# Transposes of the softmax statistics: one per step, and eight steps into the next unit for the last pair

## Chip, cores and metric

The kernel runs on one core of one Trainium2 chip. The metric is the device time of one execution in microseconds (us), median of the runs of one kernel; lower is better. The engines are named as in the profile: PE (TensorE) multiplies matrices, PEld loads its weights, DVE (VectorE), ACT (ScalarE) and POOL (GpSimd) work on tiles, SP issues the DMA transfers.

## What is computed

One layer of a decoder trunk on x (2048 rows of 1024). After an RMS norm, one input projection gives queries, keys, values, memory queries and a gate. Twelve heads of 64 in three groups attend to a dilated window each, (128, 1), (512, 4) and (2048, 16); four memory heads attend to 256 memory rows. The three groups are merged by the shares of their softmax denominators:

```python
# per group g: o (heads' outputs) and lse (log-sum-exp) of the window's scores
alpha = jax.nn.softmax(jnp.stack(lses, axis=0), axis=0)
mixed = [(outs[g] * alpha[g][..., None]) for g in range(3)]
# (mixed heads ++ memory heads) * silu(gate) -> output projection -> residual -> RMS norm
```

So for every row and head the merge needs two numbers of each group: the score's negated maximum and the sum of the exponentials. The kernel keeps them for all heads in two small tiles, `nm_all` and `l_all`.

## The kernel before

The rows are cut into four chunks of 512 (c = 0 to 3). The heads go in pairs of 64 + 64; the order is two pairs of heads of groups 2, 1, 1, 0, 0, then the stage of the memory heads, and at the end the last pair, (2,1). A pair and a chunk make a unit: the projections K, V, Q and gate one after the other, then a burst of scores and values. Each projection is 24 products of 128x512 (eight slices of the depth, three products per slice because the operands are split in a high and a low part: lines 142, 143, 144). A memory unit has only Q and gate. After the last pair comes the output phase: 16 blocks of rows, each two output projections (lines 706 to 708).

The emission is timed by steps. `run()` counts one slot for every `yield` of the projection that is being emitted; a projection is four steps of six products, so a unit is 16 steps and a memory unit 8. `at(n, f)` puts work f into the slot n later, and `steps(gen)` lets a generator go on by one part, up to its next `yield`, per slot. A tile framework then decides the final order on each engine from these emissions; all waits come from it: an instruction waits for its operands and for a free buffer. The buffers that matter are three PSUM banks `pp` (projections and transposes share them), four banks `ps` for scores, one bank `po` for values, one SBUF tile `mid` through which blocks are turned, four `p` for probabilities.

Every engine works off its own queue in order. What the change and the prediction touch:

- Scores: L401 (memory: L457) to `ps`. L379 on DVE subtracts the bias and writes a column of `nm_all`; L380 on ACT takes the exponentials and writes a column of `l_all` (memory: L462, L466, L469, then L473 on POOL). The probabilities are turned by L335 on DVE through `mid`, L338 (DMA to `t_dr`) and L344 (DMA back to `p`), and then read by the values' products, L423 or L446, into `po`. L426 takes `po` out.
- Values: V is evacuated from `pp` by L251, turned by L323 through the same `mid` and by copies L326 on ACT and POOL into `vb`. K and Q are evacuated by L251 (L290 for memory), the gate by L312.
- `shares()` is started 20 slots into the memory stage. For the six pairs done by then it transposes each group's columns of `nm_all` and `l_all` on PE into a `pp` bank (L584), copies the bank to SBUF on DVE (L586), writes it to `st_dr` in DRAM in a new order (L591, L593, L596), reads it back (L601), works out the shares in `weigh_groups` (L561 to L574) and stores them in `f_dr` (L607).
- `chunk_shares(c)` does the same for the last pair and one chunk: two transposes (L616), two copies (L617), stores (L622), a read (L629), `weigh_groups`, stores to `f_dr` (L635). It runs in the unit after the chunk's own, for the last chunk in the output phase.
- `make_y` multiplies the heads' outputs by `f_dr` (read L671, product L675, split L676 and L677) for the output products.

Of the kernel before, what the change touches and what calls it, by code (L numbers as in the profile page):

```python
# [34 lines left out]
def trunk_kernel(ctx, tc, xT, xrows, w_in, g_in, w_out, memT, mrows, g_mem, w_mem, g_fin, nbias, ident_in, out):  # L35
# [33 lines left out]
    def sb(shape, dt, tag, bufs):  # L69
        return pool.tile(shape, dt, tag=tag, name=f"{tag}_{nc.next_id()}", bufs=bufs)  # L70

    def tmp():
        return sb([P, CH], F32, "tmp", 3)

    def pbank(p=ps_p, tag="pp"):
        return p.tile([P, CH], F32, tag=tag, name=f"{tag}_{nc.next_id()}")
# [5 lines left out]
    def w_tiles():  # L82
        return sb([P, NK, P], F32R, "wh", 4), sb([P, NK, P], F32R, "wl", 4)
# [475 lines left out]
    def weigh_groups(m, f):  # L559

        v.tensor_tensor(f[:, 3, :], m[:, 0, :], m[:, 2, :], op=ALU.min)  # L561
        v.tensor_tensor(f[:, 3, :], f[:, 3, :], m[:, 4, :], op=ALU.min)
        for g in range(3):
            v.tensor_tensor(f[:, g, :], f[:, 3, :], m[:, 2 * g, :], op=ALU.subtract)
        yield
        a.activation(f[:, :3, :], f[:, :3, :], AF.Exp)
        yield
        for g in range(3):
            v.tensor_tensor(m[:, 2 * g, :], f[:, g, :], m[:, 2 * g + 1, :], op=ALU.mult)
        v.tensor_tensor(m[:, 0, :], m[:, 0, :], m[:, 2, :], op=ALU.add)  # L570
        v.tensor_tensor(m[:, 0, :], m[:, 0, :], m[:, 4, :], op=ALU.add)
        v.reciprocal(m[:, 0, :], m[:, 0, :])
        for g in range(3):
            v.tensor_tensor(f[:, g, :], f[:, g, :], m[:, 0, :], op=ALU.mult)  # L574

    def shares():

        kk = sb([P, 5 * P], F32, "kk", 2)
        vb = sb([P, 5, P], F32, "vb", 2)
        for i, src in enumerate((nm_all, l_all)):  # L580
            for g in range(3):
                n = 32 if g == 2 else 64
                pt = pbank()
                pe.transpose(pt[:n, :P], src[:, g, :n // 16].rearrange("p h b -> p (h b)"), ident)  # L584
                t = (vb[:64, 3 * i + g, :] if 3 * i + g < 5 else kk[:64, :P])
                v.tensor_copy(t[:n], pt[:n, :P])  # L586
                for h in range(n // 16):
                    dst = st_dr[2 * g + i, h]
                    s = t[16 * h:16 * h + 16, :]
                    if g == 2:  # L590
                        sp.dma_start(dst.rearrange("(r n) -> r n", r=16), s)  # L591
                    elif g == 1:
                        sp.dma_start(dst.rearrange("(j b i) -> b j i", j=4, b=16),  # L593
                                     s.rearrange("b (j i) -> b j i", j=4))
                    else:
                        sp.dma_start(dst.rearrange("(r b i) -> b r i", r=16, b=16),  # L596
                                     s.rearrange("b (r i) -> b r i", r=16))
            yield
        q = S // 32
        m = kk[:64, :6 * q].rearrange("p (s n) -> p s n", s=6)  # L600
        sp.dma_start(m, st_dr[:, :2].rearrange("s h (b n) -> (h b) s n", n=q))  # L601
        for _ in range(4):
            yield
        f = vb.rearrange("p b n -> p (b n)")[:64, :4 * q].rearrange("p (s n) -> p s n", s=4)
        yield from weigh_groups(m, f)
        yield
        sp.dma_start(f_dr[:, :2].rearrange("g h (b n) -> (h b) g n", n=q), f[:, :3, :])  # L607
        yield

    def chunk_shares(c):  # L610

        cs = slice(c * CH, (c + 1) * CH)
        t = tmp()
        for i, src in enumerate((nm_all, l_all)):
            pt = pbank()
            pe.transpose(pt[:32, :P], src[:, 2, 2:].rearrange("p h b -> p (h b)"), ident)  # L616
            v.tensor_copy(t[:32, i * P:(i + 1) * P], pt[:32, :P])  # L617
        yield
        for i in range(2):
            for h in range(2):  # L620
                b = 16 * h + 4 * c
                sp.dma_start(st_dr[4 + i, 2 + h, cs].rearrange("(r n) -> r n", r=4), t[b:b + 4, i * P:(i + 1) * P])  # L622
        q = CH // 32
        m = t[:64, 2 * P:2 * P + 6 * q].rearrange("p (s n) -> p s n", s=6)
        f = t[:64, 3 * P:3 * P + 4 * q].rearrange("p (s n) -> p s n", s=4)
        for _ in range(2):
            yield
        for h in range(2):
            sp.dma_start(m[32 * h:32 * h + 32], st_dr[:, 2 + h, cs].rearrange("s (b n) -> b s n", n=q))  # L629
        for _ in range(3):  # L630
            yield
        yield from weigh_groups(m, f)
        yield
        for h in range(2):
            sp.dma_start(f_dr[:, 2 + h, cs].rearrange("g (b n) -> b g n", n=q), f[32 * h:32 * h + 32, :3, :])  # L635
        yield
# [46 lines left out]
    def load_rows(r):  # L683
        residual[r] = row_tile("wh")
        sp.dma_start(residual[r], xr[r])
# [54 lines left out]
    def at(delay, fn):  # L740
        todo.setdefault(slot[0] + delay, []).append(fn)
# [7 lines left out]
    def steps(gen):  # L749

        def step():
            if next(gen, 0) != 0:
                at(1, step)
        at(1, step)
# [56 lines left out]
    for idx, (g, pp) in enumerate(pairs):  # L811
        if g == 3:
            ws = memory_stage()
            continue
        col = 2 * g + pp
        nbs = {}

        def load_bias(col=col):
            nbs[0] = sb([P, CH], F32, "nb", 1).rearrange("p (h k) -> p h k", h=2)
            sp.dma_start(nbs[0], nbias[col])  # L820

        if idx == 0:
            ws = [w_tiles(), w_tiles()]
            first = load_early(0)
            for k in range(NK):
                next(first)
                if k % 2 == 0:
                    load_first(ws, (6 + col, 12 + col), k // 2)
            next(first, None)
            sp.dma_start(ident, ident_in)  # L830
            ws += [load_w(w_in[t]) for t in (col, 20 + col)]
            load_bias()
        else:
            at(7, load_bias)
        following = []
        if idx < 4:
            n = 2 * pairs[idx + 1][0] + pairs[idx + 1][1]
            ahead = [6 + n, 12 + n, n, 20 + n]
        else:
            ahead = [None, 26, 18, 27]  # L840
        prev = None
        for c in range(NC):
            st = {}
            pv = prev if g == 0 else None
            if idx == 6:
                if c == 0:
                    at(6, burst)
                else:
                    at(3, lambda c=c: steps(chunk_shares(c - 1)))
                if c == 1:  # L850
                    for i in range(2 * NK):
                        at(15 * i // 8, lambda i=i: load_wo(i))
                elif c == 3:
                    for k in range(NK):
                        at(2 * k, lambda k=k: make_y(0, k))
                    for i, fn in ((6, lambda: load_rows(0)), (10, load_gfin), (11, lambda: load_rows(1))):
                        at(i, fn)

            def load_ahead():
                if c == NC - 1 and idx < 5:  # L860
                    t = ahead[len(following)]
                    following.append(load_w(w_in[t]) if t is not None else None)

            if idx == 0 and c == 0:
                first_chunk(st, ws)
            else:
                if idx == 0 and c < NC - 1:
                    steps(load_x(c + 1))
                    at(14, lambda c=c: spread_r(c + 1))
                    at(17, lambda c=c: spread_r(c + 1))  # L870
                run(proj_k(st, g, c, ws[0], pv, late=4 if (idx, c) == (0, 1) else 0))
                if (idx, c) == (4, 3):
                    steps(memory_kv(mem))
                elif (idx, c) == (4, 1):
                    steps(memory_squares(mem))
                load_ahead()
                run(proj_v(st, g, c, ws[1], pv))
                load_ahead()
                run(proj_q(st, g, c, ws[2]))
                load_ahead()  # L880
            run(proj_gate(st, g, c, ws[3], ps=st.get("gate")))
            load_ahead()
            burst((st, g, pp, c), 1, nbs[0])
            prev = st
        ws = following
    at(2, lambda: steps(chunk_shares(3)))
    for c in range(NC):
        for b in range(4):
            if c < NC - 1:
# [67 lines left out]
```

## Time and profile before

| what | value |
| --- | --- |
| time, median of 3 runs | 991.27 us (990.44 to 993.23) |
| profiled execution | 994.41 us, its span 992.3 us |
| TensorE clock granted, mean | 0.99 of full speed |
| PE busy | 961.4 us, 97% of the span |
| DVE, ACT, POOL busy | 44%, 33%, 24% |

A busy share of 97% on PE leaves little idle time in all, and the map of the profile by 40 slices shows where it is: one slice near 720 to 744 us has PE busy 60% at a granted clock of 0.7. The list of waits tells for each line what PE waited for, and the timelines show the instructions around it. A row of a timeline gives the start, the time it took, engine, line, operation and tiles, and in brackets the idle time before it and what ended it.

### The profile page before, as it was taken

The page shows a single profiled execution, that of the slowest core. Times are in us where ns is not written, and L with a number is a line of the kernel's source. Part 1 is how long each engine was busy: PE and PEld are TensorE (multiplying, and loading weights), DVE is VectorE, ACT ScalarE, POOL GpSimd, SP SyncE. Part 2 cuts the span into 40 slices and gives each one's busy share as a digit, 9 for nine tenths or more (in the row PEclk, how much of TensorE's full clock was granted, in tenths as well). Part 3 has the DMA queues.
Part 4 walks back from the last instruction along what each step waited for, and adds up shares of the span by engine and source line. Part 5 has one row for each costly group of instructions (what it writes and reads, how often), then busy time and mean ns, then how long its engine had stood idle before and what let it go on. Part 6 is the DMA issues. An engine that isn't in the chain of part 4 may idle for free. (4 is left out here: it accounts for less than half of the span.)

```text
span 992.3 us, 13998 instructions
## 1 busy us (share of the span) xinstructions
PE 961.4 (97%) x4844; PEld 755.5 (76%) x4844; DVE 436.8 (44%) x1059; ACT 326.0 (33%) x996; POOL 242.6 (24%) x393
## 2 busy tenths in 40 slices
PE   7899999999999999999999999999969999999997
PEld 5677778888788777777777876777747778888886
DVE  7866433333333333433433334543434555556333
ACT  5756422233223322233323332222333441222111
POOL 4411500032002311131112255344431310111000
PEclk9999999999999999999999999999979999999999
DMA  5565322243224423354235543333562575876311
GB/s 190 164 202 181 118 84 85 75 139 128 85 86 125 142 85 96 98 136 129 86 96 163 176 130 117 129 138 117 174 212 84 161 226 161 258 226 195 127 64 63
DMA packets 104117, 135.17 MB, mean 136 GB/s; under 512 B 31856, under 2 KB 65904, under 8 KB 104048
## 3 DMA queue, kind: packets, MB, share of 16 engines
q1 hardware_dynamic: 104048, 134.30, 42.8%
q8 instruction: 38, 0.62, 0.3%
q14 instruction: 31, 0.25, 0.1%
HBM read 89.14 MB, written 45.12 MB: 135 GB/s over the span
## 5 line engine op out<-in xcount | busy, mean ns | idle before, releaser
L142 PE MATMUL pp<-xH,wh 128*128 128x512 f32 x888 | 359.3, 405 | 0.1
L143 PE MATMUL pp<-xL,wh 128*128 128x512 f32 x888 | 354.8, 400 | 2.4 <-DVE xL L200 2.4
L144 PE MATMUL pp<-xH,wl 128*128 128x512 f32 x888 | 354.5, 399 | 1.1 <-DVE wl L80 1.1
L142 PEld LDWEIGHTS pp<-xH,wh 128*128 128x128 f32 x888 | 168.4, 190 | 49.0 <-issue 9.3
L143 PEld LDWEIGHTS pp<-xL,wh 128*128 128x128 f32 x888 | 168.4, 190 | 44.9 <-DVE xL L200 3.7
L144 PEld LDWEIGHTS pp<-xH,wl 128*128 128x128 f32 x888 | 168.2, 189 | 44.5 <-DVE wl L80 2.4
L326 POOL COPY vb<-mid 32x128 f32<-32x128 f32 (+1 forms) x208 | 60.6, 291 | 234.8 <-DVE mid L323 226.6
L326 ACT COPY vb<-mid 32x128 f32<-32x128 f32 (+1 forms) x208 | 60.7, 292 | 155.8 <-DVE mid L323 153.7
L706 PE MATMUL pp<-xH 128*128 128x512 f32 (+1 forms) x264 | 101.1, 384 | 0.2 <-ACT xH L676 0.2
L707 PE MATMUL pp<-xL,xH 128*128 128x512 f32 (+1 forms) x264 | 101.0, 383 | 0.0
L708 PE MATMUL pp<-xH,xL 128*128 128x512 f32 (+1 forms) x264 | 100.9, 384 | 0.0
L380 ACT ACTIVATE p<-p,nm_all 128x128 f32<-128x128 f32 (+1 forms) x192 | 86.2, 450 | 43.3 <-DVE nm_all L379 27.4
L80 POOL TENSOR_TENSOR wl<-wraw,wh 128x512 fp32r<-128x512 f32 x52 | 67.1, 1302 | 125.9 <-ACT wh L79 123.8
L335 DVE STREAM_TRANSPOSE mid<-p 128x1024 f32<-128x1024 f32 (+1 forms) x56 | 66.9, 1194 | 47.5 <-DMA t_dr<-mid 36.1
L473 POOL TENSOR_SCALAR p<-p,sm 128x256 f32<-128x256 f32 x64 | 58.2, 928 | 77.5 <-DVE sm L469 77.5
L312 DVE SCALAR_TENSOR_TENSOR tmp<-pp,Rb 128x512 f32<-128x512 f32 x31 | 21.4, 690 | 115.9 <-PE pp L144 110.5
L379 DVE CUSTOM_DVE_ANT_0 p<-ps,nb 128x128 f32<-128x128 f32 (+1 forms) x192 | 58.0, 360 | 7.8 <-PE ps L401 7.6
L313 ACT ACTIVATE u<-tmp 128x512 f32<-128x512 f32 x30 | 18.9, 630 | 129.2 <-DVE tmp L312 127.5
L708 PEld LDWEIGHTS pp<-xH,xL 128*128 128x128 f32 x264 | 49.6, 188 | 10.4 <-DVE xL L677 0.5
L706 PEld LDWEIGHTS pp<-xH 128*128 128x128 f32 x264 | 49.7, 188 | 10.1 <-ACT xH L676 0.4
L707 PEld LDWEIGHTS pp<-xL,xH 128*128 128x128 f32 x264 | 49.6, 188 | 9.5
L466 ACT ACTIVATE p<-ps,sm 128x256 f32<-128x256 f32 x64 | 29.5, 476 | 82.5 <-issue 46.6
(152 smaller groups left out, 844.2 us busy)
## 6 DMA issues: line engine op xcount, KB each, us to landing
t_dr<-mid SPq DMA_DIRECT2D x46, 512.0 KB
p<-t_dr SPq DMA_DIRECT2D x184, 128.0 KB
wraw<-in_w_in SPq DMA_DIRECT2D x56, 256.0 KB
wh<-in_xrows SPq DMA_DIRECT2D x16, 512.0 KB
z_dr<-u SPq DMA_DIRECT2D x30, 256.0 KB
out<-wh SPq DMA_DIRECT2D x15, 512.0 KB
Rb<-z_dr SPq DMA_DIRECT2D x24, 256.0 KB
wraw<-f_dr SPq DMA_DIRECT2D x48, 128.0 KB
```

Of the source, the lines that this page charges most:

```text
L80: on.tensor_tensor(wl, raw, wh.bitcast(F32), op=ALU.subtract)
L142: pe.matmul(ps, wh[:, k, :], xh, start=(k == 0), stop=False)
L143: pe.matmul(ps, wh[:, k, :], xl, start=False, stop=False)
L144: pe.matmul(ps, wl[:, k, :], xh, start=False, stop=(k == NK - 1))
L326: (gp.tensor_copy if (i + j) % 2 else a.copy)(dst[32 * j:32 * j + 32, :, 32 * i:32 * i + 32], mid[32 * i:32 * i + 32, :, 32 * j:32 * j + 32])
L335: v.transpose(mid.rearrange("p (j t b) -> p t j b", j=4, t=n), src.rearrange("p (t j b) -> p t j b", t=n, j=4))
L379: v.tensor_tensor_reduce(p, sc, bias, -SCALE, BIG, ALU.add, ALU.min, nm)
L380: a.activation(p, p, AF.Exp, bias=nm, scale=-1.0, accum_out=l)
L473: gp.tensor_scalar(w, w, sm[:, 1, h, b:b + 1], None, op0=ALU.mult)
L706: pe.matmul(ps, yH[:, k, bs], woH[:, k, ns], start=(k == 0), stop=False)
L707: pe.matmul(ps, yH[:, k, bs], woL[:, k, ns], start=False, stop=False)
L708: pe.matmul(ps, yL[:, k, bs], woH[:, k, ns], start=False, stop=(k == NK - 1))
```

## The change

Three edits. In `shares()` the `yield` moves into the loop over the groups, so that each slot emits one transpose with its copy and its stores, in place of three. In `chunk_shares()` the `yield` moves into the loop over the two statistics: one transpose per slot in place of two. And `chunk_shares` begins eight slots into the next unit in place of three; in the output phase seven in place of two.

```diff
                         sp.dma_start(dst.rearrange("(r b i) -> b r i", r=16, b=16),
                                      s.rearrange("b (r i) -> b r i", r=16))
-            yield
+                yield
         q = S // 32
...
             v.tensor_copy(t[:32, i * P:(i + 1) * P], pt[:32, :P])
-        yield
+            yield
         for i in range(2):
...
-                    at(3, lambda c=c: steps(chunk_shares(c - 1)))
+                    at(8, lambda c=c: steps(chunk_shares(c - 1)))
...
-    at(2, lambda: steps(chunk_shares(3)))
+    at(7, lambda: steps(chunk_shares(3)))
```

PE in the memory stage (the gate projection `pp_5465`, 594 to 602 us in the profile before): the difference of the two orders, where the six transposes of `shares()` begin.

```order
 L584 MATMUL pp_5487<-ident,nm_all 64x128
-L584 MATMUL pp_5495<-ident,nm_all 64x128
 L142 MATMUL pp_5465<-xH,wh_4850 128x512
 L143 MATMUL pp_5465<-xL,wh_4850 128x512
-L584 MATMUL pp_5503<-ident,nm_all 32x128
 L144 MATMUL pp_5465<-xH,wl_4852 128x512
 L142 MATMUL pp_5465<-xH,wh_4850 128x512
 L143 MATMUL pp_5465<-xL,wh_4850 128x512
 L144 MATMUL pp_5465<-xH,wl_4852 128x512
-L584 MATMUL pp_5519<-ident,l_all 64x128
-L584 MATMUL pp_5527<-ident,l_all 64x128
+L584 MATMUL pp_5505<-ident,nm_all 64x128
```

All six stood among the last twelve products of this projection; now three stand there, six products apart, and the other three in the next unit's Q projection, six apart too.

PE in the last pair, unit c = 1 (the stretch of 724 to 742 us before), where the statistics of chunk 0 are transposed; `pp_6632` is V, `pp_6690` and `pp_6674` are Q, `pp_6746` is the gate. Before:

```order
L446 MATMUL po_6430<-p_6160,vb_5247 64x256 x4
L143 MATMUL pp_6632<-xL,wh_6066 128x512
L144 MATMUL pp_6632<-xH,wl_6068 128x512
L446 MATMUL po_6430<-p_6183,vb_5247 64x256 x4
L616 MATMUL pp_6645<-ident,nm_all 32x128
L616 MATMUL pp_6649<-ident,l_all 32x128
L142 MATMUL pp_6690<-xH,wh_6235 128x512
```

Now:

```order
L144 MATMUL pp_6674<-xH,wl_6237 128x512
L401 MATMUL ps_6800<-kk_6588,q_6736 128x128
L401 MATMUL ps_6802<-kk_6588,q_6736 128x128
L401 MATMUL ps_6800<-kk_6588,q_6736 128x128
L401 MATMUL ps_6802<-kk_6588,q_6736 128x128
L401 MATMUL ps_6800<-kk_6588,q_6736 128x128
L401 MATMUL ps_6802<-kk_6588,q_6736 128x128
L401 MATMUL ps_6800<-kk_6588,q_6736 128x128
L446 MATMUL po_6430<-p_6183,vb_5247 64x256 x4
L401 MATMUL ps_6802<-kk_6588,q_6736 128x128
L616 MATMUL pp_6714<-ident,nm_all 32x128
L616 MATMUL pp_6726<-ident,l_all 32x128
```

The whole Q projection and the unit's scores have moved ahead of the second half of the values and of the two transposes, which are still neighbours.

DVE in the same place: before,

```order
L251 TENSOR_TENSOR kk_6588<-pp_6590,Rb 128x512
L335 STREAM_TRANSPOSE mid_6426<-p_6324 128x8x4x32
L323 STREAM_TRANSPOSE mid_6471<-tmp_6447 128x512
L426 TENSOR_TENSOR u_6099<-u_6099,po_6430 128x512
L379 ISA p_6570,nm_all<-ps_6558,nb_6450 128x128
```

and now:

```order
L251 TENSOR_TENSOR kk_6588<-pp_6590,Rb 128x512
L335 STREAM_TRANSPOSE mid_6426<-p_6324 128x8x4x32
L251 TENSOR_TENSOR tmp_6668<-pp_6632,Rb 128x512
L251 TENSOR_TENSOR q_6736<-pp_6674,Rb 128x512
L426 TENSOR_TENSOR u_6099<-u_6099,po_6430 128x512
L323 STREAM_TRANSPOSE mid_6471<-tmp_6447 128x512
L379 ISA p_6570,nm_all<-ps_6558,nb_6450 128x128
```

The evacuations of V and Q of unit 1 and of the values (L426) now stand ahead of L323, and L379, whose columns of `nm_all` the transposes read, behind all of them.

PE in the last pair, unit c = 3 (787 to 791 us before); `pp_7106` is K, `pp_7154` V, `pp_7202` Q. Before:

```order
L143 MATMUL pp_7154<-xL,wh_6066 128x512
L144 MATMUL pp_7154<-xH,wl_6068 128x512
L616 MATMUL pp_7169<-ident,nm_all 32x128
L616 MATMUL pp_7173<-ident,l_all 32x128
L142 MATMUL pp_7154<-xH,wh_6066 128x512
```

Now:

```order
L144 MATMUL pp_7202<-xH,wl_6237 128x512
L616 MATMUL pp_7243<-ident,nm_all 32x128
L142 MATMUL pp_7202<-xH,wh_6235 128x512
L143 MATMUL pp_7202<-xL,wh_6235 128x512
L144 MATMUL pp_7202<-xH,wl_6237 128x512
L142 MATMUL pp_7202<-xH,wh_6235 128x512
L143 MATMUL pp_7202<-xL,wh_6235 128x512
L144 MATMUL pp_7202<-xH,wl_6237 128x512
L616 MATMUL pp_7261<-ident,l_all 32x128
```

The two have left the V projection (after its first six products) for the Q projection, after 12 and 18 of its 24. In unit c = 2 it is the same.

## Rows read from the trace of the kernel before

**Rows 1.** The profile's page: busy time by engine, share of the span, instructions.

```profile
PE 961.4 (97%) x4844; PEld 755.5 (76%) x4844; DVE 436.8 (44%) x1059; ACT 326.0 (33%) x996; POOL 242.6 (24%) x393
```

**Rows 2.** Waits of PE: what waited for what, us in all, times, the longest.

```profile
PE pp L616 <- DVE nm_all L379: 5.4, 1, 5.4
PE pp L616 <- DVE kk L251: 3.1, 2, 1.7
PE po L446 <- POOL xL L653: 2.8, 1, 2.8
...
PE pp L584 <- DVE vb L586: 2.1, 1, 2.1
...
PE pp L616 <- ACT p L380: 0.7, 1, 0.7
```

**Rows 3.** Stretches: length; busy of PE, PEld, DVE, ACT, POOL; PEclk; DMA; GB/s.

```profile
595.00:600.00 5.00, 2.88 (x11) 1.98 (x11) 3.03 (x7) 0.00 (x0) 3.58 (x4) 0.76 0.12 11
...
730.00:735.00 5.00, 0.00 (x0) 0.00 (x0) 3.87 (x18) 4.23 (x18) 2.29 (x8) 0.58 0.54 173
735.00:740.00 5.00, 4.02 (x11) 2.94 (x11) 3.29 (x9) 2.46 (x10) 1.28 (x1) 0.50 0.64 233
...
810.00:815.00 5.00, 4.75 (x21) 3.19 (x20) 4.47 (x18) 3.11 (x12) 0.00 (x0) 1.00 0.36 110
```

**Rows 4.** Timeline of PE, memory stage: start, length, instruction [idle before <-releaser].

```profile
593.93 0.39 PE L144 MATMUL pp<-xH,wl 128*128 128x512 f32 x1
594.16 0.38 PE L584 MATMUL pp<-ident,nm_all 128*64 128x128 f32 x2
...
597.12 0.28 PE L584 MATMUL pp<-ident,nm_all 128*32 128x128 f32 x1 [2.13 <-DVE vb L586]
...
598.19 0.63 PE L144 MATMUL pp<-xH,wl 128*128 128x512 f32 x1
598.61 0.63 PE L584 MATMUL pp<-ident,l_all 128*64 128x128 f32 x2
...
601.57 0.65 PE L446 MATMUL po<-p,vb 128*64 128x256 f32 x4
```

**Rows 5.** Timeline of DVE, memory stage.

```profile
595.01 1.25 DVE L335 STREAM_TRANSPOSE mid<-p 128x1024 f32<-128x1024 f32 x1 [1.36 <-POOL p L473]
...
596.79 0.47 DVE L586 COPY vb<-pp 64x128 f32<-64x128 f32 x2
```

**Rows 6.** Timeline of SP, issues of the loads of probabilities after the transposes.

```profile
608.68 0.83 SPq L344 DMA_DIRECT2D p<-t_dr  x2
```

**Rows 7.** Timeline of PE, the values' products after those loads.

```profile
621.25 1.08 PE L446 MATMUL po<-p,vb 128*64 128x256 f32 x8
```

**Rows 8.** Timeline of PE, last pair, unit c = 1.

```profile
728.81 1.08 PE L446 MATMUL po<-p,vb 128*64 128x256 f32 x8 [2.77 <-POOL xL L653]
735.31 0.40 PE L616 MATMUL pp<-ident,nm_all 128*32 128x128 f32 x1 [5.42 <-DVE nm_all L379]
736.37 0.40 PE L616 MATMUL pp<-ident,l_all 128*32 128x128 f32 x1 [0.66 <-ACT p L380]
...
740.54 1.29 PE L446 MATMUL po<-p,vb 128*64 128x256 f32 x8
```

**Rows 9.** Timeline of DVE, the same stretch.

```profile
729.92 0.71 DVE L323 STREAM_TRANSPOSE mid<-tmp 128x512 f32<-128x512 f32 x1 [8.38 <-DMA t_dr<-mid]
730.56 0.65 DVE L426 TENSOR_TENSOR u<-u,po 128x512 f32<-128x512 f32 x1
```

**Rows 10.** Timeline of DVE, unit c = 2.

```profile
759.85 1.25 DVE L335 STREAM_TRANSPOSE mid<-p 128x1024 f32<-128x1024 f32 x1 [0.53 <-ACT p L380]
761.02 0.65 DVE L251 TENSOR_TENSOR kk<-pp,Rb 128x512 f32<-128x512 f32 x1
```

**Rows 11.** Timeline of PE, output phase.

```profile
810.85 0.28 PE L616 MATMUL pp<-ident,nm_all 128*32 128x128 f32 x1
...
812.12 0.29 PE L616 MATMUL pp<-ident,l_all 128*32 128x128 f32 x1
```

## Prediction

> **What bounds the kernel now.** I read the page first: PE is busy for 961.4 of 992.3 us [rows 1], so a change can only give what PE idles, or what it runs at the lower clock. The list of PE's waits comes next, because it names the lines. The transposes of the statistics carry most of it: L616 waits 5.4 us for L379, 3.1 us in two waits for L251 and 0.7 us for L380, and L584 waits 2.1 us for its own copies L586 [rows 2]. That is 11.3 us at instructions that take 0.3 to 0.4 us each. Third, the stretches: around two of these waits the granted clock falls, to 0.76 in 595 to 600 and to 0.58 and 0.50 in 730 to 740 [rows 3], so the products behind them are slow too. Last, the timelines of PE and DVE at each place, for what stands ahead of the awaited instruction. The reader is to see in them that a transpose on PE is short, and that it waits in PE's only queue, with all projections behind it.
>
> Two prices are used throughout. At full clock one product takes 0.23 us from start to start (593.93 to 594.16), at the half clock 0.42 (598.19 to 598.61) [rows 4]. A transpose has 128 columns where a product has 512, so I estimate 0.06 us for it.
>
> **Part 1, one transpose per step in the memory stage.** From the first transpose at 594.16 to the values at 601.57 PE needs 7.41 us [rows 4] for 12 products and 6 transposes, which at full clock are 12 x 0.23 + 6 x 0.06 = 3.1 us. So 4.3 us are lost: 2.1 idle, the rest to the lower clock. The cause: three banks, and the third transpose needs one that the first copy L586 frees. That copy starts at 596.79, behind L335, which began at 595.01 after a wait of 1.36 us for POOL [rows 5]. DVE's order ahead of the copy stays. Now PE has two times six products between first and third transpose and reaches the third at 594.16 + 12 x 0.23 + 2 x 0.06 = 597.04; the first of the two copies ends at 596.79 + 0.24 = 597.03. The wait is gone or 0.1 to 0.2 us, and with it the fall of the clock. The last three transposes cost 3 x 0.06 in the next Q projection. The sixth needs the fourth's copy, which stands behind another L335 that can be held by the turning tile's DMA: I give it 0.2, between 0 and 1. Sum: 4.3 - 0.2 - 0.2 = 3.9 us gained, at best 4.3.
>
> What may eat it is what comes after. PE gets ahead of the loads. The loads L344 of the next probabilities were issued from 608.68 on [rows 6] and read at 621.25 [rows 7], 12.6 us later. PE is now about 4 us earlier, and the new order has these values 13 products (3.0 us) further forward: 5.4 us remain from the first issue. It should be enough but is close; the stores of the statistics stand on SP's queue beside these loads, now spread over more steps. Between 602 and 720 us the list of PE's waits has none of note, so what is gained here should stay gained until 720.
>
> **Part 2, the last pair, unit c = 1.** Here the transposes are not parted: the order puts Q of unit 1 and its eight score rows ahead, then the second half of the values, then both transposes. Before, PE idled 2.77, 5.42 and 0.66 us from 726.04 (728.81 - 2.77) on [rows 8], in all 8.85. The chain is DVE's: L323 waited 8.38 us for the turning tile, ran at 729.92, then L426, the scores' L379 and ACT's L380 [rows 9]. From L323 to the first transpose are 735.31 - 729.92 = 5.4 us, to the second 6.45.
>
> Now, on the clock of before: Q fills 726.04 + 24 x 0.23 = 731.6; its evacuation on DVE (0.7, with handing over about 0.9) to 732.5; seven score rows about 0.9; the values' second half 1.08 [rows 8], to 734.5; L426 0.65 [rows 9] and L323 can start at about 735.3, because DVE has L426 ahead of it and that waits for PE. L426 now stands ahead of L323, so the first transpose follows L323 by 5.4 - 0.65 = 4.75 (740.1), the second by 6.45 as before (741.8): the ACT chain has no L426 in it. PE goes on at 742.2. Before it went on at 736.8 and still had Q (5.5) and the scores (1.06) to do: 743.4. Gain 1.2 us. The stall keeps its size nearly (about 7.7 for 8.85), and the half clock behind it (0.58 and 0.50 [rows 3]) too. The bounds: nothing, if L323 has to wait for its DMA again or L379 for ACT; 2.8, if only the wait for the loads at 728.81 vanishes whole. I take 1.2.
>
> **Part 3, units c = 2 and 3.** Both second transposes wait for a bank that L251 of K frees. In c = 2 that L251 ran at 761.02, straight behind L335 of 759.85 [rows 10]; PE had just finished K. After the change 12 and 18 products of Q and all of V lie between K's end and the transposes, 36 x 0.23 = 8.3 us. The banks they take are K's and V's, emptied 2 us or more before. In c = 3 the shares of chunk 1 now stand on DVE between K's and V's evacuation (fifteen short instructions and an exponential between them, 2 to 3 us by my estimate), and V's bank still comes free before PE has done the 18 products. Gain 3.1 us, the whole of the two waits, and no fall of the clock is involved.
>
> **Part 4, output phase.** The two transposes move from the first block to the second. Before, they cost PE next to nothing (810.85 and 812.12 [rows 11]); I take 0, between 2 us lost and 0.4 gained. The cover is the store of finished pieces: if DVE's pieces L677 come late, PE waits, since nothing else is left to run.
>
> A rule on the clock is weighed here. The trace: around the two lone transposes of the output phase the granted clock is 1.00 [rows 3, 11]. The Trainium skill, "TensorE: Matmul & The Clock Gate", section "Part 4: PE-mode transpose", states that transposes don't count as activity for the clock as products do, which would speak against strewing them among products; what that would cost is the last rival below.
>
> **Sum** on the profiled execution: 3.9 + 1.2 + 3.1 = 8.2, 994.41 - 8.2 = 986.2. The median of the runs is 3.1 us below the profiled one, so the forecast is 991.27 - 8.2 = 983.1.
>
> **Rivals.**
> 1. Unit c = 1 keeps or worsens its stall. For it: L323 must have the turning tile, and that wait was the longest on DVE [rows 9]. Against: its DMA was done at 729.9, and L323 is due 5 us after that. From 0 to 2 us lost instead of 1.2 gained: 984.3 to 986.3. I take 985.3.
> 2. Part 1's gain is given back at the loads [rows 6, 7] or at the sixth transpose. For it: 5.4 us from issue to use, on a queue shared with the stores. Against: the order lets the stores spread too. The gain left is 1.2 + 3.1 = 4.3: 987.0.
> 3. The stalls only move: gains of parts 1 to 3 are real where they stood, but PE meets the loads and the turning tile sooner, in the memory stage and in unit 1. What is then left is about 1 to 2 us: 989.5, no change that can be told.
> 4. Slower: DVE's queue in unit c = 3 and the first output block. The copies L617 there stand behind the shares of the chunk before and behind the pieces L675 and L677, and these wait for DMAs from `f_dr`; the gate projection or the next output block needs the bank that the copy frees. A wait of the size in unit 1 (5.42 and a half-clock stretch: 736.37 to 740.54 for nine products [rows 8], 4.2 - 9 x 0.23 = 2.1 more) costs 7.5; two of them, 15. From more than 8.2 on it decides; with two the time is 991.27 - 8.2 + 15 = 998. Against: the banks are needed 12 products (2.8 us) after the copy's transpose.
> 5. The clock falls at every lone transpose: 30 products in the memory stage and 6 in each of four chunks at 0.42 for 0.23, 54 x 0.19 = 10.3 us. 991.27 - 8.2 + 10.3 = 993.4. Rows 3 and 11 speak against it.
>
> **Chances.** Forecast 0.53 (its own range 980.5 to 985), rival 1 0.14, rival 2 0.13, rival 3 0.11, rival 4 0.06, rival 5 0.03. The range of 978.5 to 990 takes in rivals 1 to 3, and below the forecast the better ends (0.4 in part 1, 1.6 in part 2, 0.4 in part 4, and the scatter of the three runs, about 2). A difference under 0.3%, 3 us, can't be told from none: same is 988.3 to 994.2. Faster: 0.53 + 0.14 and most of rival 2, 0.79; same 0.13; slower 0.08.
>
> **What would show it.** In the new profile's waits, L584 has 0.3 us or less, and L616 no longer waits for L251; L616 still waits 4 to 7 us for L379 and L380 in unit 1, and the granted clock still falls behind it. 595 to 605 us is at clock 1.00. L446 has no wait in the memory stage (rival 2: one of 2 to 4 us), and L251, L711 and L706 to 708 wait under 1 us in all (rival 4: 5 or more). The forecast is wrong if L616's wait in unit 1 is gone, since then the chain of part 2 was misread, or if new waits of more than 3 us stand in the list.

## The result and the profile after

The changed kernel takes 984.94 us (median of 4 runs, 983.32 to 985.45), the kernel before, beside it on the same chip, 991.40 (4 runs, 990.44 to 993.23). The ratio is 0.9933, interval 0.9916 to 0.9949: 6.5 us faster. The forecast was 983.1, with a range of 978.5 to 990. The profiled execution of the changed kernel is the 985.45 one, with a span of 983.4 us.

PE's waits after (waiting line, what it waited for: us in all, times, the longest):

```profile
PE pp L616 <- DVE nm_all L379: 5.2, 1, 5.2
...
PE pp L706 <- ACT xH L676: 1.4, 1, 1.4
PE pp L616 <- ACT p L380: 1.1, 1, 1.1
...
PE ps L401 <- DVE q L251: 0.9, 1, 0.9
```

Against [rows 2] three things are gone: the wait of L584 for L586, the two of L616 for L251, and the one of L446 for the loads of the probabilities (rows 2 put it down to L653; the profiles of e3 and e8 below put it down to the DMA `p<-t_dr`). The longest one stays, at about its old size. Small ones have come or grown: 0.9 us at L401, 1.4 at L706 (0.2 before) and 1.1 for L380 (0.7 before).

The stretches (length; busy of PE, PEld, DVE, ACT, POOL; PEclk; DMA; GB/s), to be held against [rows 3]:

```profile
595.00:600.00 5.00, 4.94 (x28) 3.44 (x28) 3.75 (x7) 0.63 (x1) 4.27 (x5) 1.00 0.19 39
600.00:605.00 5.00, 5.00 (x32) 3.27 (x29) 3.72 (x7) 2.93 (x13) 1.56 (x2) 1.00 0.38 121
...
730.00:735.00 5.00, 0.00 (x0) 0.00 (x0) 3.66 (x19) 4.10 (x17) 2.30 (x8) 0.96 0.01 2
735.00:740.00 5.00, 3.89 (x10) 2.92 (x11) 2.27 (x18) 4.98 (x25) 1.29 (x1) 0.50 0.63 227
740.00:745.00 5.00, 5.00 (x23) 3.18 (x23) 2.42 (x3) 1.22 (x4) 0.00 (x0) 0.85 0.39 145
...
760.00:765.00 5.00, 5.00 (x35) 3.78 (x34) 1.75 (x8) 0.15 (x1) 0.82 (x1) 1.00 0.23 69
```

In the memory stage PE is busy throughout at clock 1.00, where it was busy 2.88 of 5 us at 0.76. Unit c = 1 is as it was: five idle microseconds, then products at 0.50.

PE in the memory stage (start, length, instruction), which answers to [rows 4]:

```profile
594.67 0.27 PE L584 MATMUL pp<-ident,nm_all 128*64 128x128 f32 x1
596.16 0.27 PE L584 MATMUL pp<-ident,nm_all 128*64 128x128 f32 x1
597.81 0.28 PE L584 MATMUL pp<-ident,nm_all 128*32 128x128 f32 x1
598.15 1.17 PE L446 MATMUL po<-p,vb 128*64 128x256 f32 x8
...
603.89 0.27 PE L584 MATMUL pp<-ident,l_all 128*64 128x128 f32 x1
```

The first three transposes are 1.5 and 1.65 us apart, with six products between each two; the values follow at once, and the other three stand in the next projection. From the first transpose to the values PE needs 3.48 us; before it was 7.41.

PE in unit c = 1, against [rows 8], and then DVE in the same stretch, against [rows 9]:

```profile
727.27 1.13 PE L401 MATMUL ps<-kk,q 64*128 64x128 f32 x14 [0.87 <-DVE q L251]
728.32 1.08 PE L446 MATMUL po<-p,vb 128*64 128x256 f32 x8
...
735.03 0.40 PE L616 MATMUL pp<-ident,nm_all 128*32 128x128 f32 x1 [5.20 <-DVE nm_all L379]
736.51 0.39 PE L616 MATMUL pp<-ident,l_all 128*32 128x128 f32 x1 [1.09 <-ACT p L380]
```

```profile
729.46 0.69 DVE L426 TENSOR_TENSOR u<-u,po 128x512 f32<-128x512 f32 x1 [2.33 <-PE po L446]
730.06 0.70 DVE L323 STREAM_TRANSPOSE mid<-tmp 128x512 f32<-128x512 f32 x1
```

L426 now stands ahead of L323, and L323 waits for it and no longer for its DMA. From L323 to the first transpose are 4.97 us (forecast 4.75), to the second 6.45 (forecast 6.45). PE idles 0.87 + 5.20 + 1.09 = 7.16 us, for 8.85 before and about 7.7 forecast.

Units c = 2 and 3 show no wait at L616 any more; PE's timeline has one pair as

```profile
760.81 0.27 PE L616 MATMUL pp<-ident,nm_all 128*32 128x128 f32 x1
762.30 0.27 PE L616 MATMUL pp<-ident,l_all 128*32 128x128 f32 x1
```

What is new stands late in the output phase, on PE, ACT and SP:

```profile
855.86 0.50 PE L706 MATMUL pp<-xH 128*128 128x512 f32 x1 [1.37 <-ACT xH L676]
```

```profile
855.19 0.62 ACT L676 CAST xH<-kk 128x512 fp32r<-128x512 f32 x1 [4.69 <-DMA kk<-z_dr]
```

```profile
847.39 1.05 SPq L668 DMA_DIRECT2D kk<-z_dr  x1
```

The piece that PE waits for was asked for 7.8 us before ACT could convert it, and PE had been idle for 0.7 us when ACT began and for 1.37 when the piece was ready.

### The profile page after: what moved, and what is told of

Its sections match the earlier page's. It is cut to its first block, busy times and chain, and to the rows that moved or that the text cites. A ratio compares the mean times of both kernels' runs of the same rounds, so it can differ in the third digit from the quotient of the medians.

```text
span 983.4 us, 13989 instructions
## 1 busy us (share of the span) xinstructions
PE 957.1 (97%) x4844; PEld 751.8 (76%) x4844; DVE 433.5 (44%) x1059; ACT 325.7 (33%) x996; POOL 241.4 (25%) x393
## 5 line engine op out<-in xcount | busy, mean ns | idle before, releaser
L142 PE MATMUL pp<-xH,wh 128*128 128x512 f32 x888 | 358.3, 404 | 1.1 <-ACT wh L79 0.7
L142 PEld LDWEIGHTS pp<-xH,wh 128*128 128x128 f32 x888 | 167.7, 189 | 51.8 <-issue 9.9
L706 PE MATMUL pp<-xH 128*128 128x512 f32 (+1 forms) x264 | 101.2, 384 | 1.5 <-ACT xH L676 1.4
L708 PE MATMUL pp<-xH,xL 128*128 128x512 f32 (+1 forms) x264 | 100.7, 384 | 0.0
L380 ACT ACTIVATE p<-p,nm_all 128x128 f32<-128x128 f32 (+1 forms) x192 | 86.1, 450 | 41.8 <-DVE nm_all L379 25.9
L335 DVE STREAM_TRANSPOSE mid<-p 128x1024 f32<-128x1024 f32 (+1 forms) x56 | 66.9, 1194 | 54.4 <-DMA t_dr<-mid 38.0
L379 DVE CUSTOM_DVE_ANT_0 p<-ps,nb 128x128 f32<-128x128 f32 (+1 forms) x192 | 57.5, 360 | 7.8 <-PE ps L401 7.6
L706 PEld LDWEIGHTS pp<-xH 128*128 128x128 f32 x264 | 49.6, 188 | 11.9 <-ACT xH L676 1.8
L708 PEld LDWEIGHTS pp<-xH,xL 128*128 128x128 f32 x264 | 49.6, 188 | 10.1 <-issue 0.3
```

The source lines that it names most:

```text
L142: pe.matmul(ps, wh[:, k, :], xh, start=(k == 0), stop=False)
L335: v.transpose(mid.rearrange("p (j t b) -> p t j b", j=4, t=n), src.rearrange("p (t j b) -> p t j b", t=n, j=4))
L379: v.tensor_tensor_reduce(p, sc, bias, -SCALE, BIG, ALU.add, ALU.min, nm)
L380: a.activation(p, p, AF.Exp, bias=nm, scale=-1.0, accum_out=l)
L706: pe.matmul(ps, yH[:, k, bs], woH[:, k, ns], start=(k == 0), stop=False)
L708: pe.matmul(ps, yL[:, k, bs], woH[:, k, ns], start=False, stop=(k == NK - 1))
```

## Experiments

Edits are against the changed kernel. Medians stand with the lowest and the highest run; the ratio is to the kernel before in the same batch. e1 to e4 shared one chip, e5 to e8 another, e9 to e11 a third; before was 991.25, 991.29 and 991.14 there. The changed kernel ran in none of these batches, so it is held against them by the ratios.

**e1, the memory stage alone.** Part 1 of the change without the last pair.

```diff
# in chunk_shares
-            yield
+        yield
...
-                    at(8, lambda c=c: steps(chunk_shares(c - 1)))
+                    at(3, lambda c=c: steps(chunk_shares(c - 1)))
...
-    at(7, lambda: steps(chunk_shares(3)))
+    at(2, lambda: steps(chunk_shares(3)))
```

> Only the edit in shares(): one transpose per step there, the last pair as before. Theory (the gains add, and what the memory stage gives is not taken back later): 991.4 - 4 = 987.4 us, between 986.5 and 988.5; L584 waits under 0.5 us, the clock from 595 to 605 us is 1.00, and the waits of L616 (5.4, 0.7, 3.1) stay as they are. Rival (the stall in unit 1 of the last pair is set by the DMA through the turning tile, so that it grows by what the memory stage gives): 990.5 to 991.5 us, and the idle time of PE in unit 1 grows from 8.9 to 12 or 13 us.

986.99 (5 runs, 986.59 to 988.02), ratio 0.9959 [0.9947, 0.9971]. The waits of L616 are those of before (5.4, 3.1, 0.7), that of L584 is gone, and L446 waits 1.6 us for the loads in unit 1 where before it waited 2.8. Alone this half is worth 4.3 us.

**e2, the last pair alone.** The other half.

```diff
# in shares
-                yield
+            yield
```

> Only the edits for the last pair: its two transposes one per step and five steps later, shares() as before. Theory (the gains add): the rest of the measured gain, 6.5 - 4 = 2.5 us by the medians or 5 us by the profiles, so 986.5 to 989; L584 waits 2.1 us as before and the clock falls to 0.76 in 595 to 600; L616 has no wait for L251, but one of about 5 for L379 in unit 1. Rival (all of the gain is here): 985 us.

987.00 (6 runs, 986.25 to 988.10), ratio 0.9959 [0.9947, 0.9970]. The waits for L251 are gone, L379 is at 5.6 and L380 at 1.1. What was not expected: L584 waits 0.3 us only, though up to 720 us nothing is different from the kernel before. The two halves give 4.3 + 4.3 = 8.5 us apart (4.26 and 4.25) and 6.5 together. The account further below, drawn up for these two profiles as well, shows where: from the transposes on they lie 3.7 and 4.2 us under e8 (the kernel before, below), the changed kernel 6.2. Of the 1.7 us between, 1.5 are in the last pair up to K of unit 3 (1.2 and 4.4 apart, 4.1 together): e1 shortens the wait for the loads in unit 1, and e2 takes it away whole, so most of it is counted twice. The other 0.4 is the memory stage, where the profile of the changed kernel has the late landing that e3 and e8 show and that of e1 has not.

**e3 and e8, the kernel before again,** with other executions profiled.

> The kernel before once more, for a second profile. The profiled execution of before took 994.41 us, 3 us above its median, and the profiles differ by 9.0 us where the medians differ by 6.5. If the 994.41 was only a slow execution, this profile takes 990.5 to 992 us and shows where the 3 us were; if the waits at the transposes are smaller in other executions, PE's waits at L584 and L616 add up to 8 to 9 us in place of 11.3; if they are the same 11.3, the 3 us lie elsewhere.

> One more look at the kernel before. In both of its profiles the DMA of the turning tile issued at 582 us let L335 start at 586.6 and 587.1, and the third transpose L584 waited 2.1 and 2.3 us (994.4 and 994.8 us in all). In the profile with only the last pair changed, whose instructions are the same up to 720 us, L335 started at 584.3 and the wait was 0.3. Theory (the wait of part 1 exists only in executions with the late landing): if L335 starts at about 584.5 here, the wait is 0.3 and the execution takes 990 to 991.5; if at about 587, 2.1 to 2.3 and 994 to 995. Rival (the wait has nothing to do with that landing): any other pairing.

e3 has a median of 991.61 (12 runs, 989.84 to 994.76), ratio 1.0005 [0.9992, 1.0017]; its profiled execution took 994.76. e8 is one execution of 991.04. PE in the memory stage, first of e3 and then of e8:

```profile
594.49 0.38 PE L584 MATMUL pp<-ident,nm_all 128*64 128x128 f32 x2
597.64 0.28 PE L584 MATMUL pp<-ident,nm_all 128*32 128x128 f32 x1 [2.32 <-DVE vb L586]
...
602.09 1.08 PE L446 MATMUL po<-p,vb 128*64 128x256 f32 x8
```

```profile
593.88 0.38 PE L584 MATMUL pp<-ident,nm_all 128*64 128x128 f32 x2
595.00 0.29 PE L584 MATMUL pp<-ident,nm_all 128*32 128x128 f32 x1 [0.28 <-DVE vb L586]
...
597.88 1.08 PE L446 MATMUL po<-p,vb 128*64 128x256 f32 x8
```

The same program waits 2.32 us in one execution and 0.28 in the other. Ten microseconds earlier stands what differs; DVE of e3 and of e8:

```profile
587.13 1.25 DVE L335 STREAM_TRANSPOSE mid<-p 128x1024 f32<-128x1024 f32 x1 [4.13 <-DMA t_dr<-mid]
```

```profile
584.49 1.25 DVE L335 STREAM_TRANSPOSE mid<-p 128x1024 f32<-128x1024 f32 x1 [2.10 <-DMA t_dr<-mid]
```

The store of the turning tile landed 2 us later, DVE's queue moved with it, and the copies L586 came after PE needed their banks. The execution that the prediction was read from (994.41) was of the late kind (L335 at 586.61), and its wait of 2.13 us is there only in such executions: in the six profiles with the old order of the memory stage, L584 waits 2.1 and 2.3 us in the two late ones and 0.3 in the four early ones (e2, e5, e6, e8). So e8, not that one, is the execution to hold the medians against.

**e5 and e6, the two halves of the last pair:** e5 only later (8 and 7 in place of 3 and 2, no `yield` inside), e6 only parted (`yield` inside, 3 and 2 kept).

> The kernel before with the later start alone: chunk_shares eight slots into the next unit (seven in the output phase), both transposes still in one step; shares() as before. The last pair's edits together gave 4.25 us by the medians (987.0 for 991.25). Theory (the place does it, the step between the two transposes nothing): 987 us, between 986.3 and 988.3, with no wait of L616 for L251 in units 2 and 3 and one of about 5 for L379 in unit 1. Rival (the parting of the two does it): 989.5 to 991.

> The kernel before with one transpose per step in chunk_shares alone, still three slots into the unit. The second transpose then stands six products (1.4 us) after the first, and before the change it waited 1.3 to 1.7 us for the bank that L251 of K frees. Theory (units 2 and 3 need either edit, unit 1's part only the later start): the two waits are gone or 0.3 us, unit 1 stays as before with 2.8, 5.4 and 0.7, so 991.25 - 2.5 = 988.7, between 988 and 989.7. Rival (the place does it all): 990.5 to 991.5.

e6: 988.17 (12 runs, 985.89 to 991.15), ratio 0.9965 [0.9953, 0.9977], the forecast of the theory. No wait for L251; in unit 1 L379 has 4.5 us, the loads at L446 still 3.2, L380 0.7. e5 missed: 990.24 (12 runs, 987.92 to 992.88), ratio 0.9990 [0.9978, 1.0001]. Its profiled execution is its fastest, 987.92, about the 987 expected; in it L335 starts early (585.10) and the waits for L251 are gone too, so the later place removes them as the parting does. The median lies where the rival (only the parting counts) put it, 989.5 to 991, but that rival would have kept these waits. Its runs lie between 987.9 and 992.9, and the late landing could account for that; but one execution of them was profiled, so the miss is not explained.

**e4, unit c = 1 later.** If the stall in unit 1 is PE coming too early to its transposes, these belong behind more projections.

```diff
-                    at(8, lambda c=c: steps(chunk_shares(c - 1)))
+                    at(15 if c == 1 else 8, lambda c=c: steps(chunk_shares(c - 1)))
```

> The changed kernel, with the transposes of chunk 0 fifteen steps into unit 1 in place of eight (the other chunks at eight): they then stand in the K projection of unit 2, and the gate of unit 1 runs while L379 and L380 finish. Theory (unit 1's stall is PE's place in the queue and nothing else; 5.2 + 1.1 + 0.9 us idle and 2 us at half clock): 985 - 8.5 = 976.5 us, between 975 and 979, L616's waits under 0.5 us and the clock in 725 to 745 at 1.00. Rival (DVE's chain L426, L323, L379 and the turning tile bound unit 1, and PE meets another wait for it, at the values or at the next bank): 982 to 985 us, with 3 us or more of new waits at L446, L401 or L142 between 725 and 770.

980.45 (4 runs, 979.04 to 980.80), ratio 0.9887 [0.9874, 0.9900]: 4.5 us under the changed kernel, where 8.5 were expected and 975 to 979 was the range. The stall is 0.62 us, and the granted clock 1.00 from 715 to 770. But PE meets two banks of projections that DVE has not emptied (PE's timeline of e4):

```profile
737.10 0.28 PE L616 MATMUL pp<-ident,nm_all 128*32 128x128 f32 x1 [0.62 <-DVE nm_all L379]
...
742.88 0.50 PE L142 MATMUL pp<-xH,wh 128*128 128x512 f32 x1 [1.48 <-DVE kk L251]
...
757.76 0.50 PE L142 MATMUL pp<-xH,wh 128*128 128x512 f32 x1 [2.03 <-DVE q L251]
```

3.5 of the 4 us that are missing are these two waits. They are of the kind that the rival named, at L142, though its time (982 to 985) was missed too.

**e7, unit 1 later and every pair further apart** (e4, and three empty steps between the transposes of a pair: `for _ in range(3 * (1 - i)): yield`, which moves later lines down by 2).

> The kernel with chunk 0's transposes fifteen slots into unit 1, and in addition three empty steps between the two transposes of a chunk, so that they fall into two projections and no projection has to take the bank that the one before it has just filled. In the trace with fifteen slots alone PE waited 0.6 for L379, 1.5 for L251 of K (in V of unit 2) and 2.0 for L251 of Q (in the gate of unit 2). Theory (those two waits come from two transposes within one projection): both go, 980.45 - 3.5 = 977 us, between 976 and 978.5. Rival (DVE's chain L653, L335, L323 bounds units 1 and 2, and PE meets it elsewhere): 979.5 to 981.

984.24 (6 runs, 982.51 to 984.80), ratio 0.9923 [0.9911, 0.9936]: no better than the changed kernel, and above both ranges that were expected. Both waits for L251 are gone, and from the memory stage's first bank of transposes (594.12) to K of unit 3 (761.98) PE takes 167.9 us, where e4 took 171.6 (594.28 to 765.85). From there to the output half block of the account below it takes 51.1, where e4 took 44.5: 6.6 lost for 3.7 gained (one of PE's four waits of this kind, the stretch, and SP's queue):

```profile
794.83 0.50 PE L708 MATMUL pp<-xH 128*128 128x512 f32 x1 [2.37 <-ACT xH L678]
```

```profile
795.00:800.00 5.00, 5.00 (x15) 3.82 (x16) 3.67 (x10) 3.00 (x15) 0.00 (x0) 0.66 0.97 222
```

```profile
778.28 0.80 SPq L637 DMA_DIRECT2D f_dr<-tmp  x2
...
781.56 1.11 SPq L673 DMA_DIRECT2D wraw<-f_dr  x2
```

The empty steps delay the shares of chunk 0, and with them their store L637 (L635 in e4, there at 771.47 us) to 778.28, while PE is early. The first output pieces need `f_dr` of that chunk, and their loads stand behind the store on SP's queue. PE then waits 5.6 us in four places, with the clock at 0.66 in 795 to 800. The cover that part 4 named is thin: in the output phase little but the pieces' products is left for PE to run.

**e9, the output phase's pair back at 2,** in the changed kernel, and **e10, the same in e4.**

> The changed kernel with the last chunk's transposes back at two slots into the output phase in place of seven. The changed kernel's trace has a wait of 1.4 us at 855.9 us for a cast of L676, whose piece had been loaded late, which before had not. Theory (PE meets the loads of the pieces too early because it gained 10 us before; the place of the last transposes has nothing to do with it): 985 us, between 984 and 986, with a wait of L706 for L676 of 0.8 to 1.8 us again. Rival (the later stores and loads of the last shares push the pieces' loads back on SP's queue): the wait is 0.3 or less and the time 983.5.

> The kernel with chunk 0 fifteen slots into unit 1 (980.45 us) and the last chunk's transposes at two slots in the output phase. If the place of the last transposes makes the wait of 1.4 us there: 979 us; if PE's lead makes it: 980 to 981, no difference that can be told.

e9: 983.52 (6 runs, 982.25 to 984.82), ratio 0.9918 [0.9903, 0.9933]; L706 waits 0.6 us for 1.4, between the two expectations. The interval overlaps that of the changed kernel, so the medians don't settle it. e10: 981.01 (5 runs, 979.90 to 982.89), ratio 0.9894 [0.9879, 0.9910], no gain over e4; its wait of 1.4 us at 851.19 is gone, and one of 1.2 us stands at 795.83 in its place. The account's last stretch below shows that the place does count: it takes 156.65 to 157.38 us in the seven profiles that start at two (before, e1, e3, e6, e8, e9, e10) and 157.86 to 159.30 in the six that start at seven (the changed kernel, e2, e4, e5, e7, e11). In e10 the gain is lost just ahead of it: 45.90 us from K of unit 3 to the output half block, where e4 takes 44.52.

**e11, the mixture:** e4, with the three empty steps for chunks 1 and 2 only, so that the store of chunk 0's shares stays early (`range(3 * (1 - i) if c in (1, 2) else 0)`).

> The kernel with chunk 0 fifteen slots into unit 1, both its transposes within one projection as in the run of 980.45 us, and three empty steps between the two transposes of chunks 1 and 2 alone. With the empty steps for all chunks the waits in units 1 and 2 went (PE 3.7 us earlier at unit 3), but the pieces for the output phase came late, 5.6 us of waits of L708 for L678, and the time was 984.2. Theory (what was late there hung on chunk 0's shares, now four steps earlier; the wait of 2.0 for L251 of Q goes): 978.5 to 979.5. Rival (the pieces' own chain of loads is the bound in unit 3, whatever came before): 980.5 to 984, with 3 us or more of waits for L678.

979.34 (4 runs, 979.14 to 980.88), ratio 0.9881 [0.9865, 0.9897], the fastest here: 12 us under before, about 5 under the changed kernel by the ratios, and about 1 under e4, which is not settled. From its waits:

```profile
PE pp L142 <- DVE kk L251: 1.5, 1, 1.5
...
PE pp L710 <- DVE xL L679: 1.1, 2, 0.7
...
PE pp L708 <- ACT xH L678: 1.0, 2, 0.7
```

The wait for the bank of q is gone, and the pieces cost 2.1 us in four waits (L708 and L710 are L706 and L708). The store of chunk 0's shares is issued at 770.14 again, and the 5.6 us at L708 are down to 1.0, which bears out what was read from e7.

## Why the prediction was right, and where its sizes were not

For the account I took the start of the same product in each profile (PE's timeline) and the us from one to the next:

| stretch, from one product to the next | before, profiled at 994.41 | before, e8 at 991.04 | after |
|---|---|---|---|
| transposes of the memory stage to the next projection | 11.85 | 8.44 | 7.71 |
| from there to the last product of V, unit 1 | 119.51 | 119.44 | 118.00 |
| from there to K of unit 3 | 55.05 | 55.53 | 51.39 |
| from there to a half block of the output phase (825.47, 822.15, 815.10) | 44.77 | 44.73 | 43.31 |
| from there to the last half block | 156.78 | 156.75 | 158.30 |

Gained against the first profile: 4.14, 1.51, 3.66, 1.46, and 1.52 lost: 9.25. Against e8: 0.73, 1.44, 4.14, 1.42, and 1.55 lost: 6.18, beside 6.5 between the medians.

**Part 1 (3.9 forecast) is the step that was mis-sized.** In the execution it was read from it came out as said: 7.41 us became 3.48, 3.9 less, with the clock at 1.00. But the sum then took "the median of the runs is 3.1 us below the profiled one" as a constant to be subtracted from both kernels. e8 shows that these 3 us are, for the most part, the wait itself: held against an execution of the median's length the stage gains 0.7. The changed kernel's own profile has the late landing too, with L335 at

```profile
587.28 1.25 DVE L335 STREAM_TRANSPOSE mid<-p 128x1024 f32<-128x1024 f32 x1 [4.11 <-DMA t_dr<-mid]
```

and neither L584's wait nor a fall of the clock. The account's first stretch in all thirteen profiles, by the order of the memory stage and by the landing:

| first stretch | early landing (L335 at 584.3 to 585.4) | late landing (586.6 to 587.3) |
|---|---|---|
| order of before | 8.44 to 8.47 (e2, e5, e6, e8) | 11.85 (before), 12.04 (e3) |
| new order | 7.33, 7.34 (e1, e4, e7, e9, e11) | 7.40 (e10), 7.71 (after) |

So what part 1 does is take the landing's lateness out of the time: the stage gains 4.1 us or more where the landing is late, and 1.1 where it is early. The 1.4 us up to 720 were not forecast. They come with the order: the second stretch takes 118.00 to 118.04 us in the seven profiles with the new one and 119.44 to 119.52 in the six with the old. Most are at the memory scores (line, operation, names, shapes, count | busy us, mean ns | idle), 602 to 722 us, e8 and then after:

```profile
L457 PE MATMUL ps<-kk,q 64*128 64x256 f32 x84 | 15.4, 400 | 0.0
```

```profile
L457 PE MATMUL ps<-kk,q 64*128 64x256 f32 x86 | 14.1, 398 | 0.0
```

About 1.3 us less for about as many records, in e1 as well (82 in 13.6) but not in e2 (82 in 15.2). The timelines show the place. Sixteen score products stand in three pieces in e8, with values and projection products between them (first fence), and in one piece in the changed kernel (second):

```profile
628.31 0.70 PE L457 MATMUL ps<-kk,q 64*128 64x256 f32 x2
628.94 1.08 PE L446 MATMUL po<-p,vb 128*64 128x256 f32 x8
629.95 1.13 PE L457 MATMUL ps<-kk,q 64*128 64x256 f32 x6
...
631.68 1.55 PE L457 MATMUL ps<-kk,q 64*128 64x256 f32 x8
```

```profile
629.78 2.00 PE L457 MATMUL ps<-kk,q 64*128 64x256 f32 x16
```

From the start of each piece to the next other instruction the three take 0.63 + 1.06 + 1.48 = 3.17 us, the one 1.93. No run tested this by itself.

**Part 2 (1.2 forecast, bounds 0 and 2.8)** was read rightly: the turn of L426 and L323, the 4.75 and 6.45 us, the wait for the loads that vanishes, the stall that stays with its half clock. By idle time it is 8.85 - 7.16 = 1.7. By the account, 3.66 less the first wait for L251 (1.3 us) leaves 2.3 (2.8 against e8).

**Part 3 (3.1 forecast)** holds: both waits are gone, 1.46 us in unit 3 by the account, and e6, which keeps the rest of unit 1 as it was, gains 3.1 by its median (2.5 by the account, against e8).

**Part 4 (0 forecast, bounds 2 lost and 0.4 gained)** came out at 1.5 lost, of which L706's wait is 1.37. It is the wait named there, at ACT's conversion of the piece rather than at L677. The condition that L251, L711 and L706 to L708 wait under 1 us in all was not met: 0.9 and 1.4, 2.3 in all. The profiles with the last pair's start at two and at seven put most of the loss down to the later place (see e9 and e10).

So the sum of 8.2 is 9.0 between the two profiled executions (994.41 and 985.45) and 6.5 between the medians. Against e8, part 1 gave about 2.2 in place of 3.9 (0.7 in its own stage, 1.4 at the scores behind it), parts 2 and 3 together 5.6 in place of 4.3, and part 4 took 1.5 in place of nothing. That the forecast of 983.1 lies within 2 us of the median is in part luck: the surplus of parts 2 and 3, and a gain at the scores that nobody forecast, stand against what part 1 and part 4 fell short.

**The rivals.** Rival 1 (unit 1 worse) fell: the second wait for DMA didn't come. Rival 2 (part 1 given back at the loads) fell: L446 has no wait in the memory stage. Rival 3 (stalls only move) is there in small: 0.9 at L401 and 1.4 at L706, not 7; e4, e7 and e10 show it growing as PE gets further ahead. Rival 4 (slower by DVE and the pieces) stayed below its point of decision in this kernel, but it is what stopped e7. Rival 5 (the clock falls at lone transposes) fell: 595 to 605 and 760 to 765 are at 1.00 with lone transposes in them. The Trainium skill, "TensorE: Matmul & The Clock Gate", section "Part 4: PE-mode transpose", says that transposes don't count as activity for the clock as products do; in the changed kernel transposes that stand alone between six products left the clock at 1.00 in 595 to 610, 760 to 765 and 785 to 790 us, so these runs show no cost of it.

## What to carry to other kernels

A wait read from one execution is priced for that execution: where its time lies 3 us off the median, take a second profile before the difference is carried as a constant. A short instruction in a queue that everything runs through belongs behind as much other work as its input needs to arrive, and no later: e4's seven more steps brought 4.5 us, e7's further parting took nearly all of it back. Each stall removed brings PE earlier to the next bank or piece, so ask which one that is and how far ahead it is emptied.

## What the runs showed of the hardware

The same 512 KB store (128 x 1024 f32, `t_dr<-mid`), issued at 582.23 us in e3 and 581.60 in e8, released L335 at 587.13 and 584.49: 4.9 and 2.9 us after its issue. In the late kind the last microsecond is nearly empty of traffic (a stretch of the changed kernel):

```profile
586.00:587.00 1.00, 1.00 (x8) 0.67 (x5) 0.00 (x0) 0.00 (x0) 0.00 (x0) 1.00 0.06 25
```

A share of 0.06 is what one of the 16 DMA engines alone would make; which engines moved is not shown here. Of the thirteen profiles four are late (before, after, e3, e10) and nine early. Both kinds stand on the same chip, e3 beside e1, e2 and e4, and e10 beside e9 and e11, so the chip alone doesn't decide it. Why the store is late in some executions was not found. Through the wait behind it, the late landing makes most of the 3.7 us between two executions of one program, on two chips (994.76 and 991.04): 3.6 us lie in the memory stage (12.04 and 8.44). With the new order a late landing costs 0.1 to 0.4 us there (7.40 and 7.71 for 7.33).
